# Attention loads reordered on one DMA queue, and one wide tile for a pair's outputs

## The chip, the cores and the metric

The program runs on one core of a Trainium2 chip. That core has a matrix engine (TensorE, PE in the profile, with its weight loads shown as PEld), a vector engine (VectorE, DVE), a scalar engine (ScalarE, ACT), GpSimd (POOL), and SyncE (SP), which here does nothing but issue DMA transfers. Each engine works through its own list of instructions strictly in order. Semaphores tie the lists together. The metric is the device time of one execution in microseconds (us), lower being better, as a median of several runs.

## The reference

Two layers of a diffusion backbone over 1024 latent tokens (a 16 by 64 grid, model width 1024) with 256 context tokens. Layer 0 mixes by Fourier transforms and long convolutions. Layer 1, where the change lies, is neighbourhood attention with 16 heads of 64 channels, and its core is this:

```
q, k, v = split(u_lat @ w_qkv);  kc, vc = split(u_ctx @ w_qkv[:, D:])
s_loc = q . k(8 rows x 32 columns around) * 64**-0.5 + bias      # masked outside the window
s_ctx = q . kc * 64**-0.5
p = softmax(concat(s_loc, s_ctx));  o = p_loc @ v + p_ctx @ vc
h = h + g1 * (o @ w_out);  h = h + g2 * swiglu(modulate(rms_norm(h)))
```

Both layers end with a SwiGLU feed-forward part; the result is the latent stream after a last RMS norm. The arithmetic is kept near float32 by splitting operands in a high part and a rest ("wh" and "wl" for weights), so that one product takes three matmuls.

## The kernel before

**Tiles and buffers.** Everything stands as 128 partitions by a free dimension. Buffers come from pools with a fixed number of slots: S4 (21 slots of 128x1024 float32), S2 (35 of 128x512), G (4), T (6), TK (4), and the tag "ws" (4 slots of 128x1024) in which raw weights arrive from DRAM before `split` turns them into wh (ScalarE, L350) and wl (VectorE, L352), which have two slots each. A load cannot be issued until its slot is free.

**Who sets the order.** The Python program writes the instructions in one order. A scheduler then decides each engine's final order: it simulates the program and issues what is ready, earlier instructions first. Loads without a data dependency can therefore move far ahead of the place where they were written, as far as free slots allow. `follow(ins)` pins order: what is written inside it, on the engine of `ins`, comes behind `ins` on that engine. It is an order of issue alone and waits for no result. `ld` issues a load on SP's queue, `ldr` on POOL's.

**The attention stage.** `attention` (L2378) runs over 64 items (8 pairs of heads x 2 halves of the query rows x 2 heads x 2 groups of columns). An item has three stages: scores on TensorE, softmax, and output (probabilities times values). In loop pass k the stages of items k-1, k-2 and k-3 are written, and between them slices of `attn_prep`, which computes keys and queries of a later pair on TensorE. The share of `attn_prep` in each pass is fixed, 1/24 of a pair's work per stage, running five stages ahead. `follow` pins TensorE to that order. Per pair, `attn_prep` does key products for pieces pc 0, 1 and 2 (8 steps each), then query products for pc 0 and 1. On its way it requests the pair's query weights (L2340, step 6 of the keys' second piece), the next pair's key weights (L2354, step 3 of the queries' second piece), and five groups of value loads (`value`, L2310; four loads in a group, one or two in the last). Each group is then scaled to 16 bit on ScalarE (L2326).

Each item loads its bias tables: even items in two G tiles, odd items in one "ws" tile. TensorE reads them last in the item's transposes (L2460). In the first 48 items the transposition of the context probabilities is left to a transposing DMA on SP's queue (L2456, `s<-tk`), which reads a TK tile that GpSimd finishes (L2455); the item's output stage reads what it delivers. The normalized outputs of four items are collected in a 128x512 tile `osb` (S2, one per half), turned and stored to DRAM by `attn_out`.

While the last pair is at work there is no next pair to prepare. Instead, `first_part` of the output projection runs between the items. Its `load_o` brings the stored outputs back from DRAM into S4 tiles on SP's queue (L2726 and L2729). Its weights come on POOL's queue into "ws".

Of the kernel before, what the change touches and what calls it, by code (L numbers as in the profile page):

```python
# [18 lines left out]
P = 128  # L19
# [239 lines left out]
class Builder:  # L259
    def __init__(self, ctx, tc, a, out, taps=None, stop=None):  # L260
        self.tc, self.nc, self.a, self.out = tc, tc.nc, a, out
        self.taps, self.stop = taps, stop
        ent = ctx.enter_context
        self.cp = ent(tc.tile_pool(name="cp", bufs=1))
        self.p4 = ent(tc.tile_pool(name="p4", bufs=21))
        self.p2 = ent(tc.tile_pool(name="p2", bufs=35))
        self.pg = ent(tc.tile_pool(name="pg", bufs=4))
        self.pt = ent(tc.tile_pool(name="pt", bufs=6))
        self.pko = ent(tc.tile_pool(name="pk", bufs=4))
        self.pw = ent(tc.tile_pool(name="pw", bufs=2))  # L270
        self.pp = ent(tc.tile_pool(name="pp", bufs=6, space=bass.MemoryType.PSUM))
        self.pq = ent(tc.tile_pool(name="pq", bufs=2, space=bass.MemoryType.PSUM))
        self.dr = ent(tc.tile_pool(name="dr", bufs=1, space=bass.MemoryType.DRAM))
        self.pad(self.cp, PAD_C)
        self.k = self.mk = self.pk = 0
        self.mj = self.p3 = 0
        self.held = False
        self.turned_hi = None
        self.banks = 8
        self.sq = {}  # L280

# [2004 lines left out]
    def attn_prep(self, pr, u):  # L2286

        nc, a = self.nc, self.a
        kk = [self.S4(F32R), self.S4(F32R)]
        kc = self.S2(F32R)
        qs, vt = {}, []

        def lin(wh, wl, pc, acc, view=lambda x: x):
            acc[pc] = self.PQ()
            for kb in range(KB):
                for w, part in ((wh, 0), (wh, 1), (wl, 0)):
                    self.mm(acc[pc][:, :WID[pc]], w[:, kb * P:(kb + 1) * P], view(u.ap(part, kb, pc)),  # L2300
                            kb == 0 and w is wh and part == 0, kb == KB - 1 and w is wl)
                yield WID[pc] / 1024

        def by_chunk(x):
            return x.rearrange("p (r h c) -> p h r c", r=8, h=4)

        vt[:] = [self.S2(F16, 1024) for _ in range(5)]
        filled = []

        def value():  # L2310
            c = len(filled)
            filled.append(c)
            st = self.T()
            n = 8 if c < 4 else 4
            if c < 4:
                src = self.vd[0:LAT].rearrange("(g r w) c -> r w g c", g=4, r=4)
                for r in range(4):
                    self.ld(st[r * 32:r * 32 + 32].rearrange("p (g c) -> p g c", g=4),
                            src[r, KSTART[c]:KSTART[c] + 32, :, pr * P:(pr + 1) * P])
            else:  # L2320
                self.ld(st[:, :256].rearrange("p (j c) -> p j c", j=2),
                        self.vd[LAT:LAT + CTX, pr * P:(pr + 1) * P].rearrange("(j p) c -> p j c", j=2))
            blocks = lambda x, w, b0, k: x[:, b0 * w:(b0 + k) * w].rearrange("p (b c) -> p b c", c=w)
            t = vt[c]
            nc.gpsimd.memset(blocks(t, 65, 0, n)[:, :, 64:65], 1.0)
            nc.scalar.activation(blocks(t, 65, 0, n)[:, :, :64], blocks(st, 64, 0, n), AF.Copy, scale=self.vs)  # L2326
            for b0, k, lo in self.low_parts(vt, c):
                nc.vector.scalar_tensor_tensor(blocks(lo, 64, 0, k), blocks(st, 64, b0, k), self.vs,
                                               blocks(t, 65, b0, k)[:, :, :64], op0=MUL, op1=SUB)

        if pr == 0:
            self.aw = self.weights(a["wk"][0])
        acc = {}
        wk = self.aw
        for pc in (0, 1, 2):
            for i, s in enumerate(lin(*wk, pc, acc)):
                if i == 3:
                    value()
                if pc == 1 and i == 6:
                    wq = self.weights(a["wq"][pr])  # L2340
                yield s
            w = WID[pc]
            for hd in (0, 1):
                own, other = slice(hd * 64, hd * 64 + 64), slice(64 - hd * 64, 128 - hd * 64)
                dst = kk[hd][:, pc * 512:pc * 512 + w] if pc < 2 else kc[:, hd * 256:hd * 256 + 256]
                nc.scalar.copy(dst[own], acc[pc][own, :w])
                nc.vector.tensor_tensor(dst[other], acc[pc][own, :w], dst[own].bitcast(F32), SUB)
        nxt = None
        for pc in (0, 1):
            for i, s in enumerate(lin(*wq, pc, acc, by_chunk)):  # L2350
                if i == 3:
                    value()
                if pc == 1 and i == 3 and pr < 7:
                    nxt = self.weights(a["wk"][pr + 1])  # L2354
                yield s
            for hd in (0, 1):
                own, other = slice(hd * 64, hd * 64 + 64), slice(64 - hd * 64, 128 - hd * 64)
                qh, ql = self.S2(F32R), self.S2(F32R)
                nc.scalar.mul(qh[own], acc[pc][own], 0.125)
                nc.vector.scalar_tensor_tensor(ql[own], acc[pc][own], 0.125, qh[own].bitcast(F32), op0=MUL, op1=SUB)  # L2360
                for t in (qh, ql):
                    self.ldr(t[other].bitcast(F32), t[own].bitcast(F32))
                qs[(hd, pc)] = (qh, ql)
        self.aw = nxt
        self.prep[pr] = (qs, kk, kc, vt)
        yield 0.1

    def attn_load(self, pr):

        qs, kk, kc, vt = self.prep[pr]  # L2370
        for hf in (0, 1):
            osb = {}
            for hd in (0, 1):
                for c0 in (0, 2):
                    yield self.attn_item(pr * 2 + hd, hd, hf, c0, qs[(hd, hf)], kk[hd], kc[:, hd * 256:hd * 256 + 256], vt,
                                         osb, pr if hd == 1 and c0 == 2 else None, 8 * pr + 4 * hf + 2 * hd + c0 // 2 < 48)
# [33 lines left out]
    def attn_item(self, head, hd, hf, c0, qs, kk, kc, vt, osb, out, cross):  # L2410

        nc, a = self.nc, self.a
# [37 lines left out]
        if cross:  # L2450

            turns.pop(1)
            x, pts[0] = self.TK(F16, 1024), self.S2(F16, 1024)
            nc.scalar.copy(x[:, :512], pc)
            nc.gpsimd.tensor_tensor(x[:, 512:], pc, x[:, :512], SUB)  # L2455
            nc.sync.dma_start_transpose(pts[0].rearrange("p (n c) -> p n c", c=P), x)  # L2456
        for k, src, n in turns:
            ps = self.PS()
            for j in range(n):
# [5 lines left out]
            pts[k] = t  # L2465
        yield
        o = self.PS()
        if hf not in osb:
            osb[hf] = self.S2()
        for i in (0, 1):  # L2470
            c = c0 + i
            ops = []
# [54 lines left out]
    def run(self):  # L2527
# [170 lines left out]
        def load_o(b, pcs, load=None):  # L2698
            for part in (0, 1):
                if 0 in pcs:  # L2700
                    t = self.S4(F32R)
                    o.put(part, b, 0, t[:, :512])
                    o.put(part, b, 1, t[:, 512:])
                for pc in pcs:
                    (load or self.ldr)(o.ap(part, b, pc).bitcast(F32), self.od[b][part][:, pc * 512:pc * 512 + 512])
# [13 lines left out]
        def first_part(pc):  # L2719
            for nb in range(KB):  # L2720
                with self.follow(self.last_mul if pc and nb > 1 else None):
                    wh, wl = self.weights(a["w_out2"][nb, :, :768], 768, load=None if pc else self.ldr)
                acc = self.PQ() if pc == 0 else self.PS()
                for kb in range(6):
                    if pc == 0 and nb == 0:
                        load_o(kb, (0,), self.ld)  # L2726
                        yield 1
                    if pc == 0 and nb == 4 + kb // 3:
                        load_o(kb, (1,), self.ld)  # L2729
                    if kb == 2:  # L2730
                        if pc or nb == 0:
                            load_h2(nb, pc)
                        if pc == 0 and nb < 7:
                            load_h2(nb + 1, pc)
                    for w, part in ((wh, 0), (wh, 1), (wl, 0)):
                        self.mm(acc, w[:, kb * P:(kb + 1) * P], by_row(o.ap(part, kb, pc)),
                                kb == 0 and w is wh and part == 0, kb == 5 and w is wl)
                    yield 0.5
                add_h(nb, pc, acc)
# [160 lines left out]
```

## Time and profile before

| | us |
|---|---|
| median of 3 runs (2869.44 to 2878.66) | 2874.7 |
| the profiled execution, its own time | 2879.49 |
| its span, first to last instruction | 2877.7 |
| TensorE busy | 2777.6 |
| VectorE busy | 2046.4 |
| ScalarE busy | 1319.4 |
| GpSimd busy | 541.2 |

A row of the profile names an instruction group by its engine, its source line and `out<-in` (the tiles written and read, numbers left out). A "q" behind an engine's name means its sequencer: SPq is the queue of SyncE. In a timeline, a row has the start, the duration, the instruction and how many were merged, and in square brackets how long the engine stood idle before it and what ended that idle time. In a table by windows, PEclk is the clock that the throttle granted TensorE, as a share of full speed. For a DMA, "to landing" is the time from its issue until its data has arrived.

### The profile page before, as it was taken

The page shows a single profiled execution, that of the slowest core. Times are in us where ns is not written, and L with a number is a line of the kernel's source. Part 1 is how long each engine was busy: PE and PEld are TensorE (multiplying, and loading weights), DVE is VectorE, ACT ScalarE, POOL GpSimd, SP SyncE. Part 2 cuts the span into 40 slices and gives each one's busy share as a digit, 9 for nine tenths or more (in the row PEclk, how much of TensorE's full clock was granted, in tenths as well). Part 3 has the DMA queues.
Part 4 walks back from the last instruction along what each step waited for, and adds up shares of the span by engine and source line. Part 5 has one row for each costly group of instructions (what it writes and reads, how often), then busy time and mean ns, then how long its engine had stood idle before and what let it go on. Part 6 is the DMA issues. An engine that isn't in the chain of part 4 may idle for free. (4 is left out here: it accounts for less than half of the span.)

```text
span 2877.7 us, 43689 instructions
## 1 busy us (share of the span) xinstructions
PE 2777.6 (97%) x15610; PEld 2327.1 (81%) x15610; DVE 2046.4 (71%) x3531; ACT 1319.4 (46%) x2269; POOL 541.2 (19%) x880
## 2 busy tenths in 40 slices
PE   7999999999999999999999999999999899999998
PEld 4876678788898888888889888888887788888887
DVE  6666776768787888876777437777677977755556
ACT  4433335443554333333455337777665533333434
POOL 2210234241001212122020002333211122112000
PEclk9999999999999999999999999999999999999999
DMA  7356425655566665658884346877755366434763
GB/s 266 119 162 225 151 82 190 221 171 220 207 194 208 203 205 197 214 202 322 307 306 157 126 130 157 202 192 187 226 189 204 128 229 225 147 110 163 233 196 133
DMA packets 296887, 554.21 MB, mean 193 GB/s; under 512 B 81872, under 2 KB 128658, under 8 KB 296670
## 3 DMA queue, kind: packets, MB, share of 16 engines
q1 hardware_dynamic: 232318, 361.06, 40.1%
q0 software_dynamic: 61504, 185.65, 18.5%
q10 hardware_dynamic: 2848, 4.72, 0.4%
q8 instruction: 123, 2.02, 0.3%
q14 instruction: 94, 0.77, 0.1%
HBM read 405.01 MB, written 118.76 MB: 182 GB/s over the span
## 5 line engine op out<-in xcount | busy, mean ns | idle before, releaser
L1932 PE MATMUL ps<-s,s 128*128 128x512 f32 x2012 | 500.7, 392 | 5.3 <-ACT tk L1937 2.0
L1932 PEld LDWEIGHTS ps<-s,s 128*128 128x128 f32 x2012 | 380.2, 189 | 86.9 <-ACT tk L1937 2.9
L346 PE MATMUL ps<-s,wh 128*128 128x256 f32 (+1 forms) x1776 | 404.1, 332 | 6.1 <-ACT wh L350 2.6
L346 PEld LDWEIGHTS ps<-s,wh 128*128 128x128 f32 x1776 | 296.7, 191 | 41.1 <-ACT wh L350 3.5
L346 PE MATMUL ps<-s,wl 128*128 128x256 f32 (+1 forms) x888 | 266.7, 328 | 0.1
L2109 PE MATMUL ps<-s,s 128*128 128x512 f32 (+1 forms) x1000 | 259.8, 383 | 3.2 <-DVE s L352 3.1
L350 ACT CAST s<-s 128x1024 fp32r<-128x1024 f32 (+2 forms) x192 | 172.6, 926 | 192.0 <-DMA s<-d 172.9
L346 PE MATMUL pq<-s,wh 128*128 128x512 f32 (+1 forms) x848 | 259.8, 388 | 0.3 <-ACT wh L350 0.3
L352 DVE TENSOR_TENSOR wl<-ws,wh 128x1024 fp32r<-128x1024 f32 (+1 forms) x141 | 169.5, 1203 | 123.2 <-ACT wh L350 118.6
L346 PE MATMUL ps<-s,s 128*128 128x65 f16 (+4 forms) x2748 | 231.3, 235 | 15.3 <-DMA s<-tk 8.7
L352 DVE TENSOR_TENSOR s<-s,s 128x1024 fp32r<-128x1024 f32 (+2 forms) x170 | 191.0, 1155 | 58.2 <-ACT s L350 57.9
L350 ACT CAST wh<-ws 128x1024 fp32r<-128x1024 f32 (+1 forms) x141 | 144.7, 1026 | 183.5 <-PE ps L346 84.7
L350 ACT CAST s<-t 128x512 fp32r<-128x512 f32 (+2 forms) x238 | 134.0, 581 | 194.8 <-PE ps L1932 71.8
L352 DVE TENSOR_TENSOR s<-t,s 128x512 fp32r<-128x512 f32 (+2 forms) x238 | 152.0, 654 | 95.9 <-ACT s L350 77.4
L2109 PEld LDWEIGHTS ps<-s,s 128*128 128x128 f32 x1000 | 184.5, 188 | 41.2 <-DVE s L352 4.9
L1932 PE MATMUL ps<-s,wh 128*128 128x512 f32 x624 | 194.8, 390 | 0.0
L346 PEld LDWEIGHTS ps<-s,wl 128*128 128x128 f32 x888 | 165.3, 190 | 16.4 <-DVE wl L352 0.6
L337 POOL DMA_DIRECT2D d<-s x186 | 101.1, 544 | 374.2 <-DVE s L1739 92.2
L346 PEld LDWEIGHTS pq<-s,wh 128*128 128x128 f32 x848 | 151.6, 190 | 23.3 <-issue 1.2
L346 PE MATMUL pq<-s,wl 128*128 128x512 f32 (+1 forms) x424 | 161.9, 382 | 1.4 <-DVE wl L352 1.4
L2109 PE MATMUL ps<-s 128*128 128x512 f32 (+1 forms) x500 | 150.7, 385 | 0.0
L346 PEld LDWEIGHTS ps<-s,s 128*128 128x128 f32 (+1 forms) x828 | 130.2, 193 | 24.0 <-ACT t L2445 4.0
(487 smaller groups left out, 5481.7 us busy)
## 6 DMA issues: line engine op xcount, KB each, us to landing
s<-d SPq DMA_DIRECT2D x282, 256.0 KB, 4.1
d<-s POOLq DMA_DIRECT2D x170, 256.0 KB, 4.2
s<-in_down SPq DMA_DIRECT2D x150, 256.0 KB, 4.2
s<-in_ada_w POOLq DMA_DIRECT2D x64, 512.0 KB, 4.9
ws<-in_up SPq DMA_DIRECT2D x44, 512.0 KB, 3.6
d<-g POOLq DMA_DIRECT2D x86, 256.0 KB, 2.9
ws<-in_gate SPq DMA_DIRECT2D x42, 512.0 KB, 4.1
d<-tk POOLq DMA_DIRECT2D x66, 256.0 KB, 4.2
```

The source lines that it names most:

```text
L337: self.last_ldr = self.nc.gpsimd.dma_start(out, in_).ins
L346: self.last_mm = self.nc.tensor.matmul(o, l, r, start=st, stop=sp).ins
L350: self.last_hi = nc.scalar.copy(hi, src).ins
L352: self.last_lo = eng.tensor_tensor(lo, src, hi.bitcast(F32), SUB).ins
L1932: nc.tensor.matmul(ps, x[:, sl], y, start=first and j == 0 and x is wh and y is xh, stop=j == 3 and x is wl, skip_group_check=True)
L2109: m = nc.tensor.matmul(acc[j][:, c0:c1], x[:, sl], y[:, xs], start=first and k == 0, stop=last and k == 2, skip_group_check=True)
```

## The change

Five edits. The query weights are requested at step 0 of the keys' second piece instead of step 6, and the next key weights at step 0 of the queries' first piece instead of step 3 of the second; both now stand inside `follow(self.last_tr)`, `last_tr` being the last transposing DMA written by then. `value` notes its last load in `value_ld`, and the first loads of `load_o` stand inside `follow(self.value_ld)`. The two `osb` tiles of a pair (two of 128x512 from S2) become the halves of one 128x1024 tile from S4, taken at the pair's first output stage. The arithmetic is the same.

```diff
-        self.turned_hi = None
+        self.turned_hi = self.last_tr = None
...
                         self.vd[LAT:LAT + CTX, pr * P:(pr + 1) * P].rearrange("(j p) c -> p j c", j=2))
+            self.value_ld = self.last_ld
...
-                if pc == 1 and i == 6:
-                    wq = self.weights(a["wq"][pr])
+                if pc == 1 and i == 0:
+                    with self.follow(self.last_tr):
+                        wq = self.weights(a["wq"][pr])
...
-                if pc == 1 and i == 3 and pr < 7:
-                    nxt = self.weights(a["wk"][pr + 1])
+                if pc == 0 and i == 0 and pr < 7:
+                    with self.follow(self.last_tr):
+                        nxt = self.weights(a["wk"][pr + 1])
...
         qs, kk, kc, vt = self.prep[pr]
+        osb = {}
         for hf in (0, 1):
-            osb = {}
...
-            nc.sync.dma_start_transpose(pts[0].rearrange("p (n c) -> p n c", c=P), x)
+            self.last_tr = nc.sync.dma_start_transpose(pts[0].rearrange("p (n c) -> p n c", c=P), x).ins
...
-        if hf not in osb:
-            osb[hf] = self.S2()
+        if not osb:
+            t = self.S4()
+            osb.update({0: t[:, :512], 1: t[:, 512:]})
...
                     if pc == 0 and nb == 0:
-                        load_o(kb, (0,), self.ld)
+                        with self.follow(self.value_ld):
+                            load_o(kb, (0,), self.ld)
                         yield 1
```

## The prediction

> **What bounds the kernel now.** I read the page first, then the attention stage (1695 to 2160 us) by windows, then what TensorE waits for there, and last the timelines of the engines around its longest gaps.
>
> ```profile
> span 2877.7 us, 43689 instructions
> PE 2777.6 (97%) x15610; PEld 2327.1 (81%) x15610; DVE 2046.4 (71%) x3531; ACT 1319.4 (46%) x2269; POOL 541.2 (19%) x880
> ```
>
> TensorE sets the time; what isn't its work is 100.1 us of gaps, plus stretches at a lower clock. The change touches the attention stage alone. In the next table the second column is the window's length, then busy time of TensorE (matmuls, weight loads), VectorE, ScalarE, GpSimd, then TensorE's granted clock, the DMA share and GB/s.
>
> ```profile
> 1695.00:1745.00 50.00, 50.00 (x252) 42.58 (x251) 29.10 (x56) 25.04 (x44) 7.33 (x17) 1.00 0.46 135
> 1745.00:2050.00 305.00, 296.29 (x2883) 265.75 (x2882) 235.39 (x524) 237.78 (x547) 94.31 (x148) 0.99 0.78 190
> 2050.00:2100.00 50.00, 44.85 (x452) 39.60 (x451) 35.79 (x84) 33.30 (x80) 10.39 (x20) 0.93 0.82 255
> 2100.00:2160.00 60.00, 60.00 (x529) 51.79 (x526) 40.87 (x83) 33.70 (x77) 13.36 (x25) 1.00 0.56 181
> 2008.46:2013.46 5.00, 5.00 (x36) 4.57 (x37) 2.96 (x9) 2.25 (x7) 1.80 (x3) 0.66 0.94 267
> 2073.00:2078.00 5.00, 5.00 (x15) 4.32 (x16) 3.19 (x9) 3.21 (x9) 0.00 (x0) 0.50 1.00 373
> ```
>
> The gaps are 305.00 - 296.29 = 8.7 us before 2050 and 50.00 - 44.85 = 5.15 us from 2050 to 2100; before 1745 and after 2100 there are none. The last two rows are the 5 us behind the two longest gaps: a clock of 0.66 costs (1 - 0.66) x 5 = 1.7 us, a clock of 0.50 costs 2.5 us. What ended the gaps (who waited, for whom, us, times, longest), and rows of TensorE's timeline with the gap in brackets:
>
> ```profile
> PE ps L346 <- DMA s<-tk: 8.7, 7, 3.0
> PE ps L346 <- ACT t L2445: 3.8, 1, 3.8
> 1804.54 0.81 PE L346 MATMUL ps<-s,s 128*128 128x65 f16 x21 [0.55 <-DMA s<-tk]
> 1956.27 0.81 PE L346 MATMUL ps<-s,s 128*128 128x65 f16 x21 [1.45 <-DMA s<-tk]
> 2008.46 0.81 PE L346 MATMUL ps<-s,s 128*128 128x65 f16 x21 [2.97 <-DMA s<-tk]
> 2073.00 1.65 PE L346 MATMUL ps<-s,s 128*128 128x384 f32 x4 [3.80 <-ACT t L2445]
> ```
>
> Before 2050 it is a transposing load every time, about once in a pair's 50 us. SP's queue ahead of the worst one, and the chain of waits through it:
>
> ```profile
> 1990.02 1.24 SPq L2456 DMA_TRANSPOSE s<-tk  x1
> 1993.40 0.85 SPq L331 DMA_DIRECT2D g<-in_bias  x2
> 1998.87 0.38 SPq L331 DMA_DIRECT2D bias<-in_bias  x1
> 1999.52 0.75 SPq L331 DMA_DIRECT2D ws<-in_wq  x1
> 2000.37 5.28 SPq L2456 DMA_TRANSPOSE s<-tk  x2
> 2000.37 8.05 DMA s<-tk
> ```
>
> The transposing load of 2000.37 (item 41) stands behind a bias table, for which SP sat from 1994.25 to 1998.87, and behind the query weights of pair 7. It lands after 8.05 us, at 2008.42; TensorE wanted it at 2008.46 - 2.97 = 2005.49, 5.1 us after its issue. Usual landings (KB each, median us):
>
> ```profile
> bias<-in_bias SPq DMA_DIRECT2D x32, 384.0 KB, 3.2
> s<-d SPq DMA_DIRECT2D x24, 256.0 KB, 7.1
> ws<-in_wk SPq DMA_DIRECT2D x6, 512.0 KB, 4.9
> ws<-in_wq SPq DMA_DIRECT2D x6, 512.0 KB, 5.0
> s<-tk SPq DMA_TRANSPOSE x48, 4.2
> ```
>
> So 384 + 512 KB just ahead turn 4.2 us into 8.05. After 2050 the culprit is another: SP's queue, ScalarE, then the chain.
>
> ```profile
> 2050.59 1.75 SPq L331 DMA_DIRECT2D s<-d  x4
> 2053.91 7.66 SPq L331 DMA_DIRECT2D s<-d  x7
> 2063.21 0.37 SPq L331 DMA_DIRECT2D t<-d  x1
> 2064.72 0.61 ACT L2447 ACTIVATE g<-g,st 128x384 f32<-128x384 f32 x1
> 2071.70 0.51 ACT L2326 ACTIVATE s<-t,c 128x256 f16<-128x256 f32 x1 [6.37 <-DMA t<-d]
> 2063.21 8.46 DMA t<-d
> ```
>
> The last group of value loads (`t<-d`, 2063.21) stands behind the first output loads (`s<-d`) and lands 8.46 us later. ScalarE's scaling of it is next in ScalarE's list, so the softmax behind it stood still for 6.37 us, and TensorE starved for 3.80.
>
> **The change part by part.** *The weights.* Nothing is added or removed: 12 requests (six `in_wk`, six `in_wq` from 1717 on) move in SP's list. Counting the loop passes, the query weights of pair p now come behind the transposing load of item 8p-10, and the key weights of the next pair behind that of item 8p-8. For pair 7's query weights that is item 46, the second transposing load in the next fence's first row, where item 41's was still ahead of it before: seven transposing loads later. Pair 7's key weights come behind item 40's (1990.02). Being written earlier, they also come ahead of any load with a later place in the program, so their new place is just behind that load, if a "ws" slot is free. The same six requests free their slots sooner: before, a request was held for some 21 us (issue 1999.52, cast 2020.93) until its wh slot came free, and this slot was missing to the bias tables.
>
> ```profile
> 2028.93 5.97 SPq L2456 DMA_TRANSPOSE s<-tk  x2
> 2020.93 1.03 ACT L350 CAST wh<-ws 128x1024 fp32r<-128x1024 f32 x1
> 2039.14 0.82 PE L2460 MATMUL ps<-c,bias 128*128 128x128 f32 x6
> 2049.69 0.63 PE L346 MATMUL pq<-s,wh 128*128 128x512 f32 x2
> L352 DVE TENSOR_TENSOR wl<-ws,wh 128x1024 fp32r<-128x1024 f32 (+1 forms) x26 | 30.6, 1176 | 25.8 <-ACT wh L350 25.6
> ```
>
> Are they in time? Pair 7's first query product is at 2049.69. Issued at 2034.9 (end of the first row), landed 5.0 later, 1.03 for the cast and 1.18 for the rest: ready at 2042.1, 7.6 us early. If no slot is free at 2034.9, the next one comes when item 47's transposes have read its bias table (2039.14 + 0.82): ready at 2047.2, still 2.5 us early. So I cost the move itself at nothing; what hides it is the key products of the last pair. If that cover is gone, it costs what the weights are late.
>
> What it gives: without weights ahead, item 41's load has at most the 384 KB table before it. Its landing is then between the usual 4.2 and the 5.0 of a 512 KB load, under the 5.1 it had; the bounds for these seven gaps are 0 and all of 8.7, and the clock's 1.7 goes with the 2.97 gap. I take 7.4 + 1.7 = 9.1, since 5.0 against 5.1 is thin and some of the gaps may keep a part (1.3 in all).
>
> The Trainium skill ("TensorE: Matmul & The Clock Gate", the table of the two states) says that the clock falls to half after an idle window of some 3.4 us. The trace disagrees in size: a gap of 2.97 was enough for a clock of 0.66. By the page alone the 1.7 would not be in the sum, and it would give 1.7 less.
>
> *The output loads.* The 12 first loads of `load_o` now come behind the last value load. That load then lands in a few us rather than 8.46, and the 6.37 us block of ScalarE goes, with TensorE's 3.80 and 2.5 of clock: 6.3. What is late next: all 24 loads (6.3 MB) now start later, and the bias tables of items 50 and up stand among them. The bound below is a new wait as long as an output load's landing beyond a bias table's, 7.1 - 3.2 = 3.9, less the 6.37 - 3.80 = 2.6 us that ScalarE's block left without effect: 1.3. I take 6.3 - 1.5 = 4.8, bounds 2.4 and 6.3, and nothing for the 1.35 us of small gaps that follow until 2088 (5.15 - 3.80). The output projection hides the later landing of its own blocks:
>
> ```profile
> 2081.05 0.63 PE L346 MATMUL pq<-s,wh 128*128 128x512 f32 x2
> ```
>
> This is its first product. Even from 2063.21, where the last value load was so late, and with 6.3 us taken off its start, 11.5 us are left for a landing of 7.1; lateness beyond that would be paid in full.
>
> *The wide tile.* A pair takes one S4 slot instead of two S2 slots in turn. S4 has 21; in the steady state 16 hold the stage's input, 2 and 2 the keys of two pairs, so the new tile takes the last one. The keys of pair p+2 then wait for item 8p+7's scores, which TensorE's fixed order has just ahead of the product that fills them: nothing. What it gives is S2 room. The transposing loads sometimes wait for a slot that an output's store still reads:
>
> ```profile
> SPq L2456 <- DMA d<-s: 19.6, 6, 3.8
> SPq L331 <- PE ps L2460: 95.9, 35, 11.3
> ACT s L2326 <- DMA t<-d: 15.8, 9, 6.4
> ```
>
> These 19.6 us of SP's time led to no gap of TensorE (none of the gaps follows them), so I cost this at nothing, and up to 1 us of gain.
>
> **Sum.** 9.1 + 4.8 = 13.9 us. The profiled execution took 2879.49 (span 2877.7 and 1.8 around it) and would take 2865.6. It stands 4.8 above the median of the runs, 2874.7, which would become **2861**. All bounds together give a gain from 2.4 to 18.8 (8.7 + 1.7 + 6.3 + 1.1 of the small gaps + 1), so 2856 to 2872. Behind the stage TensorE is busy without a gap (2100 to 2160), so I count on the gain being kept.
>
> **The rivals.** *The load moves and the wait stays.* A weight request that finds no free slot gets the next one when an odd item's transposes end, and just then that item's own transposing load comes up: 512 KB would again stand ahead of one, only another. For it: SP waits 95.9 us for these transposes (second row above). Against it: 512 KB alone is less than the 896 before. If half of 10.4 stays, and the tail gives 2.4: 5.2 + 2.4 = 7.6, so **2867**, within the noise. By the Trainium skill ("DMA: Bandwidth & Descriptors", "Issuing engines are not separate DMA queues") the transfers of all queues share the same 16 engines. By that rule POOL's stores would still slow the transposing load, and the time would come out on this rival's side; 8.05 us beside the usual 4.2 does not tell which transfer was to blame.
>
> *Slower: ScalarE blocked by the weights.* The cast of a weight used to find its data 21 us old; now the scheduler, whose time is not the chip's, may place it right behind the simulated landing. ScalarE is in order, and a cast that waits holds up every softmax behind it. The value loads show it: nine waits of 15.8 us in all (third row), and 2.6 us of one block cost TensorE nothing. With a block b at each of 12 casts the loss is 12 x (b - 2.6). It outweighs the gain by over 0.3% from 12 x (b - 2.6) = 13.9 + 8.6, that is b = 4.5. With b = 5.0, a whole landing, it is 29 us, so **2890**. Against it: eight of the nine waits took (15.8 - 6.4) / 8 = 1.2 us.
>
> *It does less than it says.* If the bias table and SP's wait until 1998.87 alone made the transposing load late, only the tail's 4.8 is gained: **2870**.
>
> **How the numbers follow.** What this measurement can tell from no change is about 0.3%, 8.6 us. Forecast (2856 to 2865) 0.55, a larger gain 0.05, the wait stays 0.17, less than it says 0.10, blocked ScalarE or late weights 0.13. Faster by over 0.3% needs 8.6: 0.60. Same: 0.27. Slower: 0.13. The range takes the forecast, both rivals without much change and the first part of the slow one: 2852 to 2878.
>
> **What would show it.** Right: TensorE's waits for `s<-tk` fall from 8.7 to under 2 us; each `in_wq` directly follows a transposing load on SP's queue; the last value load precedes all `s<-d`; no clock of 0.50 around 2060 to 2080. Wrong: waits of `wh` L350 on `ws<-in_wq` over 2.6 us, gaps of TensorE at the first query product of a pair, or a new gap on a bias table behind the output loads.

## The result, and the profile after

The changed kernel took 2862.39 us (median of 6 runs, 2856.19 to 2867.56) beside 2875.12 us of the kernel before (6 runs on the same chip): the ratio is 0.9958, with a 95% interval from 0.9942 to 0.9975. That is 12.7 us less, where 13.7 below the median were forecast. The sum came out nearly right, but two of its terms did not, and their errors cancelled by luck. What follows shows first where the time went and then, by parts of the change, why.

The page of the changed kernel has this head:

```profile
span 2865.8 us, 43630 instructions
PE 2779.7 (97%) x15610; PEld 2325.6 (81%) x15610; DVE 2045.2 (71%) x3531; ACT 1321.0 (46%) x2269; POOL 543.2 (19%) x880
```

TensorE's gaps (span less busy time) fell from 100.1 to 86.1 us. The waits in the attention, in the same view as before (who waited, for whom, us, times, longest): one of SP's, two of ScalarE's, and three of TensorE's:

```profile
SPq L331 <- PE ps L2463: 55.1, 21, 11.2
...
ACT wh L350 <- DMA ws<-in_wk: 6.3, 6, 1.5
...
ACT s L2327 <- DMA t<-d: 5.6, 4, 3.1
...
PE ps L346 <- DVE st L2446: 2.6, 1, 2.6
...
PE ps L346 <- DVE s L2467: 1.3, 2, 1.0
...
PE ps L346 <- DMA s<-tk: 0.4, 1, 0.4
```

The wait for transposing loads, 8.7 us in seven gaps before, is one gap of 0.4. The value loads hold up ScalarE for 5.6 us in all, where it was 15.8. But a new wait has come: one gap of 2.6 us on an addition of VectorE (L2446 adds the bias table to the scores). Outside these rows TensorE waited 0.5 us for ScalarE and, behind the attention, 1.3 us for `wl`. SP's queue around items 39 to 42 shows the weights' new place:

```profile
1974.04 3.93 SPq L2459 DMA_TRANSPOSE s<-tk  x2
1978.02 0.58 SPq L331 DMA_DIRECT2D ws<-in_wq  x1
...
1989.35 1.23 SPq L2459 DMA_TRANSPOSE s<-tk  x1
1990.62 0.58 SPq L331 DMA_DIRECT2D ws<-in_wk  x1
...
1993.71 0.88 SPq L331 DMA_DIRECT2D g<-in_bias  x2
1995.12 0.38 SPq L331 DMA_DIRECT2D bias<-in_bias  x1
1995.67 1.24 SPq L2459 DMA_TRANSPOSE s<-tk  x1
```

Each request for weights directly follows a transposing load; so do all 12 from 1746 us on. Beside that, SP now goes from the `g` tables (done at 1994.59) to the next `bias` table in 0.5 us. Before, it sat there from 1994.25 to 1998.87, until a "ws" slot was free. The first row of the waits sums this up: L2463 is what L2460 was, the transposes that release an odd item's bias table, and SP's waits for them fell from 95.9 us (35 times) to 55.1 (21 times).

The table by windows of the changed kernel has the columns as before (window, its length, busy time of TensorE's matmuls and weight loads, VectorE, ScalarE, GpSimd, then TensorE's granted clock, DMA share and GB/s). The first two windows part the stage so that the second ends behind its last gap:

```profile
1745.00:2038.00 293.00, 292.23 (x2839) 259.82 (x2839) 232.45 (x519) 236.69 (x542) 94.64 (x148) 1.00 0.79 197
2038.00:2088.00 50.00, 45.90 (x465) 40.82 (x464) 37.06 (x88) 34.90 (x83) 9.34 (x18) 0.95 0.90 281
2075.00:2080.00 5.00, 4.55 (x39) 4.12 (x39) 3.62 (x9) 3.19 (x9) 0.99 (x2) 0.66 1.04 302
2086.30:2091.30 5.00, 5.00 (x42) 4.57 (x39) 3.22 (x8) 3.03 (x9) 0.00 (x0) 0.66 0.31 121
2270.00:2310.00 40.00, 39.32 (x173) 31.93 (x172) 34.66 (x55) 16.33 (x27) 9.02 (x17) 1.00 0.75 264
```

The long stretch has 0.8 us of gaps, down from 8.7. The 50 us to 2088 still lose 4.1 us in gaps, where the corresponding 50 us lost 5.15, and their clock is 0.95 (0.93 before). So the second part of the change gave almost nothing here. Its cause is in the timeline of TensorE and in the chain of waits:

```profile
2086.03 1.61 PE L346 MATMUL ps<-s,s 128*128 128x65 f16 x30 [2.60 <-DVE st L2446]
```

```profile
2074.42 10.77 DMA g<-in_bias
```

and in SP's queue ahead of that bias table:

```profile
2048.35 1.59 SPq L331 DMA_DIRECT2D t<-d  x1
2049.99 1.04 SPq L331 DMA_DIRECT2D s<-d  x2
...
2055.00 18.11 SPq L331 DMA_DIRECT2D s<-d  x20
2074.42 0.33 SPq L331 DMA_DIRECT2D g<-in_bias  x1
```

The last value load (`t<-d`, 2048.35) now goes ahead of all but one of the 24 output loads, and ScalarE's long block is gone. But 20 output loads now stand in one row, and the bias table behind them is issued only at 2074.42 and lands 10.77 us later. The row takes 18.11 us not for the issuing alone: for 8.2 us of it, in ten pieces, SP waits until an earlier output load has landed. The gap of 2.60 is followed by a stretch at half clock: 0.66 over the 5 us from 2086.3.

The last row of the windows is a surprise from outside the attention. In the feed-forward part behind it the kernel before had 4.3 us of gaps in the same 40 us, at a clock of 0.96:

```profile
2270.00:2310.00 40.00, 35.67 (x149) 28.76 (x148) 34.43 (x55) 16.32 (x27) 8.24 (x16) 0.96 0.68 237
```

### The profile page after: what moved, and what is told of

The parts are those of the page before. It is cut to its first block, busy times and chain, and to the rows that moved or that the text cites. A ratio compares the mean times of both kernels' runs of the same rounds, so it can differ in the third digit from the quotient of the medians.

```text
span 2865.8 us, 43630 instructions
## 1 busy us (share of the span) xinstructions
PE 2779.7 (97%) x15610; PEld 2325.6 (81%) x15610; DVE 2045.2 (71%) x3531; ACT 1321.0 (46%) x2269; POOL 543.2 (19%) x880
## 4 chain that ended last, share of the span: by engine, by line
PE 71%; issue 3%; DVE 3%; DMA 2%; ACT 1%; POOL 1%; DVEq 0%; SPq 0%; POOLq 0%; ACTq 0%
PE ps L1932 25%; PE ps L346 15%; PE ps L2109 11%; PE pq L346 9%; PE pq L1932 3%; PE pq L2109 3%; PE ps L2230 2%; PE ps L2463 1%; PE ps L1425 1%; DMA s<-d 1%; DMA s<-in_c_ctx 1%; DMA g<-in_bias 0%; DMA s<-in_x_t 0%; DVE wl L352 0%; DVE s L352 0%
```

## The time by stages

All kernels below do the same work, so three marks in the timeline of VectorE divide each profile: the reciprocals of the softmax in the attention's items 0, 48 and 63, which one group of instructions holds (64 of them, one per item; here before):

```profile
L2485 DVE RECIPROCAL st<-ps x64: 159/171/172, 1749.6 to 2149.2; 128x2 f32<-128x2 f32 x64
```

The first mark falls between 1743.4 and 1754.2 in the thirteen profiles, although almost nothing is changed ahead of it. The stretches at half clock in the earlier stages fall differently from one execution to the next: ahead of the first mark the clock not granted there adds up to 22.2 to 35.8 us. So one profile's span is good to some 5 us only, and the durations from mark to mark are the better measure:

| kernel | item 0 to 48 | 48 to 63 | 63 to the end |
|---|---|---|---|
| before | 304.6 | 95.0 | 728.5 |
| after: weights, outputs, tile | 294.6 | 94.3 | 722.7 |
| weights (e1) | 294.5 | 92.6 | 720.0 |
| outputs (e2) | 310.9 | 94.2 | 728.7 |
| tile (e3) | 306.5 | 89.9 | 725.2 |
| weights, outputs (e4) | 295.1 | 94.4 | 720.6 |
| weights' new place, not pinned (e5) | 305.0 | 91.8 | 726.9 |
| weights pinned, at the old place (e6) | 316.3 | 88.1 | 729.8 |
| weights on POOL's queue (e7) | 308.9 | 92.1 | 727.3 |
| bias tables pinned (e8) | 311.1 | 92.1 | 723.2 |
| after, second output loads late (e9) | 295.5 | 88.5 | 721.3 |
| weights, second output loads late (e10) | 294.2 | 89.1 | 720.7 |
| weights, tile (e11) | 295.7 | 89.4 | 722.7 |

From before to after that is -10.0, -0.7 and -5.8 us, with +4.6 ahead of the first mark: -11.9, which is 2865.8 - 2877.7.

## The experiments

Ratios are against the kernel before, run on the same chip; its median was 2875.0 to 2876.7 us in all of them.

### One part of the change at a time

**e1_weights** does the weights' move alone.

```diff
-                if pc == 1 and i == 6:
-                    wq = self.weights(a["wq"][pr])
+                if pc == 1 and i == 0:
+                    with self.follow(self.last_tr):
+                        wq = self.weights(a["wq"][pr])
...
-                if pc == 1 and i == 3 and pr < 7:
-                    nxt = self.weights(a["wk"][pr + 1])
+                if pc == 0 and i == 0 and pr < 7:
+                    with self.follow(self.last_tr):
+                        nxt = self.weights(a["wk"][pr + 1])
```

> Only the two weight requests are moved and pinned behind the last transposing load; the output loads and the two narrow output tiles are as before. My theory (a term of the prediction): this is the larger part, about 9 us less than the kernel before; TensorE's waits for the transposing loads fall from 8.7 us to under 2, and the stall of 3.80 us at the last value load and the half clock behind it stay. Rival (the wait stays, only at another transposing load): the waits keep 4 us or more and the time falls by 3 us or less.

Measured: 2856.99 us (2852.81 to 2861.07), ratio 0.9940 [0.9921, 0.9958]. This one part alone gives 18 us, more than the whole change and twice the 9.1 that the forecast gave it. Its waits for `s<-tk` are 0.3 us in all. Its gaps at the end of the attention, on TensorE's timeline:

```profile
2055.66 0.98 PE L346 MATMUL ps<-s,s 128*128 128x384 f32 x4 [1.93 <-ACT t L2447]
2062.02 1.35 PE L346 MATMUL ps<-s,s 128*128 128x384 f32 x4 [0.72 <-DVE s L2466]
2067.60 1.07 PE L346 MATMUL ps<-s,s 128*128 128x256 f32 x6 [0.36 <-DVE s L2503]
2069.65 0.59 PE L346 MATMUL ps<-s,s 128*128 128x384 f32 x2 [0.99 <-DVE s L2466]
```

The last value load stands behind output loads here as it did before, and yet the gap it leaves is 1.93 us and not 3.80, with no stretch at half clock behind it.

**e2_outputs** pins the first output loads behind the last value load, and does nothing else.

```diff
+            self.value_ld = self.last_ld
...
-                        load_o(kb, (0,), self.ld)
+                        with self.follow(self.value_ld):
+                            load_o(kb, (0,), self.ld)
```

> Only the first output loads are pinned behind the last value load. My prediction's term: about 5 us less than before, with the waits for the transposing loads still at about 8.7 us. Rival, which the profile after the change suggests: ScalarE's wait for the last value load goes (6.37 us to under 3), but a bias table that now stands behind 20 output loads takes its place, so the last part of the stage loses as much as before and the time is within 2 us of the kernel before.

Measured: 2881.53 us, ratio 1.0022 [1.0006, 1.0037], 6 us more than before. Its runs scatter more than others': two of the twelve took 2869, the other ten 2878 to 2886 us. Two of TensorE's waits in it:

```profile
PE ps L346 <- DMA s<-tk: 12.3, 7, 2.9
...
PE ps L346 <- DVE st L2444: 3.8, 1, 3.8
```

The second is the wait on the bias table, as in the changed kernel and longer; again one table (`g<-in_bias`) lands 10.70 us after its issue. Up to the first output loads the order of SP's queue is that of the kernel before, so the first row says something else: the same order cost 8.7 us of waits for transposing loads in one profile and 12.3 in another.

**e4_no_tile** is the whole change without the wide tile, that is, weights and outputs.

> The change without the wide tile. If the parts add up and the tile gives nothing: the same as the whole change, about 12 us less than the kernel before, waits for transposing loads under 2 us. Rival (the tile carries part of it): 4 us or more slower than the whole change.

Measured: 2861.54 us, ratio 0.9953 [0.9936, 0.9969], so beside the weights alone the output loads' pin loses about 4 us here too by the medians, though the two intervals overlap. In its profile the same wait on a bias table is 3.6 us.

**e3_tile** has the wide tile alone.

```diff
-        if hf not in osb:
-            osb[hf] = self.S2()
+        if not osb:
+            t = self.S4()
+            osb.update({0: t[:, :512], 1: t[:, 512:]})
```

> Only the collected outputs share one wide tile. My prediction's term: nothing, within 2 us of the kernel before, waits for the transposing loads still 7 to 10 us; SP's waits for the stores (DMA d<-s, 19.6 us) fall. Rival: the freed narrow slots let transposing loads go earlier and the tile alone brings a good part of the gain, 4 us or more.

Measured: 2875.98 us, ratio 1.0004 [0.9993, 1.0015]: nothing. Its waits for `s<-tk`, and all its gaps at the end of the attention:

```profile
PE ps L346 <- DMA s<-tk: 10.4, 8, 2.0
```

```profile
2074.20 1.36 PE L346 MATMUL ps<-s,s 128*128 128x384 f32 x4 [0.72 <-DVE s L2464]
2081.25 0.59 PE L346 MATMUL ps<-s,s 128*128 128x384 f32 x2 [0.87 <-DVE s L2464]
```

The output loads were not touched here, and the gap of 3.80 us, on which the forecast rested its second term, isn't there at all.

**e11_weights_tile** adds the tile to the weights' move.

> The weights' move and the wide tile, the output loads as before the change. Theory (the tile costs and gives nothing, with the weights moved as well as without): 2857.0 as the weights alone, within 2 us, and waits for s<-tk under 1 us. Rival (the tile takes the last free slot of the wide pool and holds back the keys of the next pair once the weights come early): a new wait of TensorE at a pair's key products, 2 to 4 us in all six pairs: 2859 to 2861.

Measured: 2856.22 us, ratio 0.9930 [0.9913, 0.9947], beside 0.9940 for the weights alone. The tile gives and costs nothing there either.

### What makes the transposing loads late

**e5_place_only** requests the weights at the earlier steps, without the pin.

```diff
-                if pc == 1 and i == 6:
+                if pc == 1 and i == 0:
...
-                if pc == 1 and i == 3 and pr < 7:
+                if pc == 0 and i == 0 and pr < 7:
```

> The kernel before with the two weight requests written at their new, earlier places but not pinned behind a transposing load. My theory, that it is the pin that counts (unpinned, a request goes out as soon as a slot is free, wherever it is written): the waits for transposing loads stay at 6 us or more and the time is within 3 us of the kernel before. Rival: the earlier place alone changes which slot the request takes and brings most of the 9 us.

Measured: 2876.32 us, ratio 1.0000 [0.9986, 1.0014]. Its SP queue at item 41, and its waits:

```profile
1998.06 0.38 SPq L331 DMA_DIRECT2D bias<-in_bias  x1
1998.72 0.91 SPq L331 DMA_DIRECT2D ws<-in_wq  x1
1999.73 5.11 SPq L2456 DMA_TRANSPOSE s<-tk  x2
```

```profile
PE ps L346 <- DMA s<-tk: 9.5, 7, 3.2
```

Here the queue is the one of before, row for row: the request still goes out as early as a slot allows, just ahead of item 41's load. Elsewhere in the stage the earlier place let the key weights change places with an odd item's bias table, in five of the pairs, and the waits stayed. It is the pin that moves a request behind the transposing load.

**e6_pin_only** pins the requests, at their old places.

```diff
                 if pc == 1 and i == 6:
-                    wq = self.weights(a["wq"][pr])
+                    with self.follow(self.last_tr):
+                        wq = self.weights(a["wq"][pr])
...
                 if pc == 1 and i == 3 and pr < 7:
-                    nxt = self.weights(a["wk"][pr + 1])
+                    with self.follow(self.last_tr):
+                        nxt = self.weights(a["wk"][pr + 1])
```

> The requests at their old places in the program, but pinned behind the last transposing load written there. My theory: most of the gain, 6 to 10 us, waits for transposing loads under 3 us; perhaps a late weight, since the request then goes out some 18 us later than in the change. Rival (pinned at the old place the weights come too late): ScalarE or TensorE waits for the weights at each pair's first query or key product, and the time is not better than before.

Measured: 2884.50 us, ratio 1.0032 [1.0018, 1.0046], 9 us slower. The waits for transposing loads are gone (0.8 us), but now the weights are late:

```profile
ACT wh L350 <- DMA ws<-in_wk: 16.5, 6, 5.3
...
PE pq L346 <- DVE wl L352: 4.9, 6, 1.4
PE pq L346 <- ACT wh L350: 2.9, 2, 1.7
```

So the earlier place is what makes up for the pin: with it ScalarE waited 1.5 us at most for the key weights (changed kernel), without it 5.3.

**e7_pool** leaves places and pins as before and requests the weights on POOL's queue.

```diff
-                    wq = self.weights(a["wq"][pr])
+                    wq = self.weights(a["wq"][pr], load=self.ldr)
...
-                    nxt = self.weights(a["wk"][pr + 1])
+                    nxt = self.weights(a["wk"][pr + 1], load=self.ldr)
```

> The kernel before with the attention's key and query weights requested on POOL's queue instead of SP's, at the same places in the program: the same bytes at about the same time, but not ahead of a transposing load on its queue. If the order on SP's queue is what delays the transposing loads: their waits fall from 8.7 us to under 3, 5 to 9 us gained. If it is the traffic as such, wherever it is issued: the landing of the worst transposing loads stays at 7 to 8 us and the waits at 5 us or more.

Measured: 2877.38 us, ratio 1.0011 [0.9999, 1.0023]: no gain. SP's queue at item 41, POOL's request, and TensorE's gap:

```profile
1993.02 1.23 SPq L331 DMA_DIRECT2D g<-in_bias  x2
1998.51 0.38 SPq L331 DMA_DIRECT2D bias<-in_bias  x1
1998.98 2.06 SPq L2456 DMA_TRANSPOSE s<-tk  x1
```

```profile
1999.59 0.56 POOL L337 DMA_DIRECT2D ws<-in_wq  x1 [3.49 <-DVE st L2485]
```

```profile
2008.11 0.81 PE L346 MATMUL ps<-s,s 128*128 128x65 f16 x21 [2.98 <-DMA s<-tk]
```

Two things remain although the weights have left SP's queue. SP still sits from 1994.25 to 1998.51 before a slot for the bias table is free (all such waits in the attention: 99.0 us). And TensorE starts on the transposing load's result only 9.1 us after its issue (1998.98 to 2008.11), although the weights were requested 0.6 us behind it and on another queue. By the Trainium skill ("DMA: Bandwidth & Descriptors", "Issuing engines are not separate DMA queues") transfers run on the same 16 engines whoever started them; these rows agree with it, but do not show that it was the weights that slowed the load.

**e8_bias_pin** leaves the weights' code as it was and pins each odd item's bias table behind the last transposing load written by then.

```diff
-            self.ld(t.rearrange("p (i k) -> p i k", i=2), a["bias"][head, hf, c0:c0 + 2].rearrange("i p k -> p i k"))
+            with self.follow(self.last_tr):
+                self.ld(t.rearrange("p (i k) -> p i k", i=2), a["bias"][head, hf, c0:c0 + 2].rearrange("i p k -> p i k"))
```

> The kernel before with the odd items' bias tables pinned behind the last transposing load written by then; the weights are as before. If the bias table ahead of the transposing load, and SP's wait for its slot, were the cause: the waits for the transposing loads fall from 8.7 us to under 3 with the weights untouched. If the weights are: they stay at 5 us or more.

Measured: 2876.93 us, ratio 1.0010 [0.9997, 1.0023]. TensorE's waits for transposing loads fell to 0.6 us. In their place stand waits that come from late bias tables (the first row is SP's wait for a slot, the second VectorE's for the tables; before, the odd items' tables held VectorE up nowhere):

```profile
SPq L331 <- PE ps L2461: 60.2, 22, 11.3
...
DVE bias L2444 <- DMA bias<-in_bias: 21.3, 14, 2.5
...
PE ps L346 <- DVE s L2465: 5.6, 10, 1.0
```

SP's waits for a slot are near the 55.1 us of the changed kernel. So without a bias table ahead that waits for its slot, the transposing loads were in time. The changed kernel seems to reach the same another way: its weights, requested later and cast as soon as they land (ScalarE waits for each `in_wk`), no longer hold the "ws" slots that the bias tables need. No run has one of the two gone and the other left whole, SP's wait and the 512 KB of weights beside the load. But the traces show how they add up at item 41. GpSimd finishes the tile that its load reads here, before and then in the changed kernel, and the third row is the landing of this one load in the changed kernel (5.5 us, where it was 8.05):

```profile
1995.14 1.17 POOL L2455 TENSOR_TENSOR tk<-t,tk 128x512 f16<-128x512 f32 x1 [5.08 <-ACT tk L2454]
...
1993.87 1.16 POOL L2458 TENSOR_TENSOR tk<-t,tk 128x512 f16<-128x512 f32 x1 [4.47 <-ACT tk L2457]
...
s<-tk SPq DMA_TRANSPOSE x1, 5.5
```

Before, the tile was ready at 1996.31, the load went out 4.06 us later (2000.37) and landed 8.05 after that, 12.1 in all; TensorE wanted it 9.2 us after the tile was ready (2005.49). In the changed kernel the tile was ready at 1995.03 and the load went out 0.64 us later (1995.67): 6.1 in all. An estimate from these rows, which takes the landing to be the same whenever the load goes out: the shorter wait alone gives 0.64 + 8.05 = 8.7, in time; the shorter landing alone 4.06 + 5.5 = 9.6, still 0.4 late. So the time on SP's queue was the larger part, and each of the two alone would have removed all or most of the 2.97 us.

### What the output loads do at the end of the attention

**e9_late_second** is the whole change, and beside it the 12 second output loads are pinned behind the last bias table.

```diff
+        self.bias_ld = self.last_ld
...
-                        load_o(kb, (1,), self.ld)
+                        with self.follow(self.bias_ld):
+                            load_o(kb, (1,), self.ld)
```

> The whole change, and beside it the 12 second output loads follow the last bias table on SP's queue. Theory (the pin of the first output loads lost time because a bias table now stands behind some 20 output loads and lands 10.8 us after its issue): the last bias tables are issued earlier, TensorE's 2.60 us wait on VectorE's add of the bias at the end of the attention and the two half-clock stretches behind it go, so 2.6 + about 2 to 3 us of clock less than the whole change's 2862.4: 2857 to 2858, beside the weights alone at 2857.0. Rival 1 (the lost time is not the bias table's): the time stays at 2861 to 2864. Rival 2 (the second output loads become late instead): TensorE waits on s<-d in the output projection, each wait up to a landing of 7 us: 2865 to 2875.

Measured: 2854.67 us (2850.45 to 2859.34), ratio 0.9925 [0.9906, 0.9943]. All the gaps of TensorE at the end of the attention, and the table by windows there:

```profile
2060.99 0.53 PE L2503 MATMUL ps<-c,s 128*128 128x128 f32 x2 [0.86 <-ACT s L2493]
2062.30 0.55 PE L2464 MATMUL ps<-c,bias 128*128 128x128 f32 x3 [0.34 <-DVE st L2447]
```

```profile
2030.00:2080.00 50.00, 48.69 (x518) 43.25 (x516) 40.96 (x97) 39.24 (x95) 9.33 (x18) 1.00 0.74 220
```

The wait on the bias table is gone, and the half clock with it; the output projection never waits for the second loads. From item 48 to 63 it takes 88.5 us where the changed kernel took 94.3. That shows the bias tables' place behind the second output loads as the cause of what the end of the attention still lost in the changed kernel. Whether a table came late by its issue or by the traffic of the loads ahead of it, this run does not tell. It gained somewhat more than the expected 2857 to 2858. By its median this is the fastest kernel measured; its interval just meets that of the changed kernel (0.9942 to 0.9975), and it cannot be told from e1, e10 and e11.

**e10_weights_late** has the weights' move and the late second loads, with the first output loads where they were.

> The weights' move alone, with the first output loads at their old place and the 12 second output loads behind the last bias table. Theory (the last value load behind the first output loads costs about 2 us and no more; the second loads stand before bias tables): the 1.93 us wait on ScalarE stays, the 0.72 and 0.99 that follow it in the weights' profile may go: 2855 to 2857, the weights alone at 2857.0. Rival (the second loads become late for the output projection): 2860 to 2870, with TensorE waiting on s<-d.

Measured: 2855.14 us, ratio 0.9928 [0.9908, 0.9948], and 89.1 us from item 48 to 63. The longest gap left there is 0.55 us; the 1.93 of e1, with the last value load again behind output loads, did not come. Beside e9 this tells that the pin of the first output loads, the change's second part, gives nothing that can be told from the noise even when its harm is taken away.

## Why the prediction was right, and where it was not

**The total** was right within 1.4 us, but by luck: it is a sum of errors that cancel.

**The weights, 9.1 us predicted.** The mechanism held at most of its steps: each request directly behind a transposing load, the waits for `s<-tk` under 2 us, one wait of 0.6 us for `in_wq`, and the request early enough. One step did not hold: "Its landing is then between the usual 4.2 and the 5.0 of a 512 KB load, under the 5.1 it had". Item 41's load landed after 5.5 us in the changed kernel and after 6.2 in e1. It was in time all the same, because it went out 0.64 us (e1: 0.80) after its tile was ready and not 4.06. The prediction left SP's wait for a slot out of this term and had it only in a rival.

Two sizes were off too. First, from item 0 to 48 the six profiles with the move take 294.2 to 295.7 us (mean 294.9), and the four in which the transposing loads were late and nothing else was moved there (before, e2, e3, e5) 304.6 to 310.9 (mean 306.8). The gain is 11.8 us; the profiled execution of before, from which 9.1 was read, was the shortest of the four. Second, "I count on the gain being kept" fell short: from item 63 to the end the same two groups take 721.3 and 727.3 us on average, another 6.0. Together that is some 18, as measured for e1.

Where do the 6.0 come from? TensorE's gaps from item 63 to the end are 18.3 us in the six and 21.8 in the four, and the clock lost is 6.4 and 9.3; together that is about the 6.0. Most of the gaps' part lies between 2270 and 2310 us (4.3 us before; none to 0.9 in the six), where TensorE waits for a copy of ScalarE (L1937), and this one for a store of an earlier result (before, then after):

```profile
ACT g L1937 <- DMA d<-g: 4.6, 1, 4.6
...
ACT g L1937 <- DMA d<-g: 0.6, 1, 0.6
```

This does not come from the weights' place as such: e8, whose weights stayed where they were written, has little of it too (0.8). What goes with it is the order that the scheduler found far behind the edit. SP's list of the feed-forward part's loads is the same in before, e2, e3, e5 and e7, which take 725.2 to 728.7 us from item 63 on. It is another one, with a single gate-weight request two places later, in the seven that take 720.0 to 723.2, e8 among them; e6 has a third order and 729.8. No run changes this order alone, so that it is the cause is likely and not shown. For the forecast it was luck.

**The output loads, 4.8 us predicted; in fact a loss of 4 to 6 by the medians.** (Only e2 beside the kernel before is clear of the noise, with an interval from 0.06 to 0.37%.) The step that failed is the price, "TensorE's 3.80 and 2.5 of clock". It came from one gap in one execution. In the four other profiles shown with the output loads at their old place and the value load behind them (e1, e3, and in the same rows of e5 and e7) ScalarE's lateness cost 1.93, 0, 1.06 and 1.48 us, and no clock. In e5 the rows of SP's queue from 2029 us to the last value load are in the very order of before, so the same order can cost 3.80 or 1.06. Against that stood what was "late next". The prediction did name it, "the bias tables of items 50 and up stand among them", but bounded it at 1.3 us by the ordinary landing of an output load, 7.1 us. It left out that SP issues one load after another and waits between them for earlier ones to land: 20 output loads took 18.11 us to go out, and the table behind them lands 10.77 us after its issue. The wait became 2.60 to 3.8 us and brought back the half clock. From item 48 to 63 the three profiles with the pin and early second loads (after, e2, e4) take 94.2 to 94.4 us; before, e1, e3, e5 and e11, without the pin, 91.7 on average. That is 2.6 of the 4 to 6 us of loss; the rest isn't located. The kernel before itself took 95.0 there, with its 3.80: in that one execution the two orders cost the same.

**The wide tile, 0 predicted.** Right, alone and with the weights (e3, e11).

**The rivals.** "The load moves and the wait stays" fell: 512 KB still stand ahead of some transposing load, but 0.4 us of waits are left. "Slower: ScalarE blocked by the weights" needed blocks of 4.5 us; they were 1.5 at most in the changed kernel and 2.6 in e1. It was no idle thought: with the pin at the old place (e6) they reach 5.3, and the kernel is slower. "It does less than it says" was half right, in that SP's wait for the bias table's slot does matter (e8); but moving the weights ends this wait too.

**What would make it wrong** had "a new gap on a bias table behind the output loads". It came, and it took the whole second term. Of the signs of being right, "no clock of 0.50 around 2060 to 2080" failed too: the clock was at half from 2076.1 to 2079.5. That the total still held is owed to the first term, and to the 6 us behind the stage, which the forecast did not have.

## What to carry to other kernels

Before a gap in one profile is priced, look whether it comes back in a second execution of the same order: what recurs in every pair (here the transposing loads) is worth its sum and more, what stands there once (the 3.80) may be luck. When loads are moved back in an in-order queue, price what stands behind them by the time that the whole row of them takes to issue and to land, not by one landing. What a transfer loses in the queue before its issue counts as much as its landing, so look when its input was ready, not only when it went out. And a request made too early costs through the buffer it holds: the weights seem to have done their harm partly in slots that bias tables were waiting for, which a move to another queue didn't cure and a later, pinned request did.

## What the runs showed of the hardware

A half-clock stretch does not follow from the length of one gap. In the changed kernel's profile the clock was at half from 2076.1 to 2079.5 behind gaps of only 0.53 and 0.97 us (and again behind the 2.60), as the row of 2075 to 2080 in its table by windows shows (0.66). In e1 a gap of 1.93 and, 12 to 14 us later, a pair of 0.36 and 0.99 went by at full clock. The Trainium skill ("TensorE: Matmul & The Clock Gate", the table of the two states) gives an idle window of some 3.4 us as the condition. The stretches here last such a window, 3.41 us, or two (6.83 from 2071.16 in the kernel before); the condition differs, since shorter gaps were enough, though not always. Between 1690 and 2330 us of the thirteen profiles, all twelve gaps of 2.60 us or more had a stretch at half clock with them. Of the shorter ones some had it (1.82 in e6, 1.91 in e7, 1.95 in e3) and others not (2.30 in e2, 2.38 in before). What decides there is not told by these runs.

The second surprise is how far the same order of instructions differs between executions: 8.7 and 12.3 us of waits for the same transposing loads (before and e2).
